# An elementwise loss kernel: its loads and stores moved from one DMA queue to three, in chunks half as large

## The chip, the cores and the metric

The kernel runs on one core of a Trainium2 chip. The metric is device time in microseconds (us); lower is better. Nearly all executions are in one undisturbed ("fast") state; the one run of an experiment that was not is named where it occurs, and two experiments had a single run each, whose state is unknown.

A core has 16 DMA engines that move data between HBM (the memory outside the core) and the on-chip SBUF, and compute engines of which two matter here: DVE (VectorE) and ACT (ScalarE). DMAs can be issued by GpSimd (called POOL in the profile), by SyncE (SP) and by ACT. Each issuer has its own queue.

## The reference

```python
# pred, target: (8192, 8192) float32; target holds 0.0 or 1.0
def reference(pred, target):
    eps = 1e-7
    pred = np.clip(pred, eps, 1 - eps)
    return -(target * np.log(pred) + (1 - target) * np.log(1 - pred))
```

As a target is 0 or 1, the result is -ln|t - 1 + p|. Each of the three arrays has 268.4 MB, and each element is used once.

## The kernel before

Each array is seen as 128 rows (partitions) of 524288 columns, and cut into chunks. A chunk of width w is a contiguous piece of HBM, so a row of it is one run of w elements: 16384 float32 values are 64 KiB. Chunks live in two rings in SBUF. The prediction tile is computed on in place and stored from there. The target load casts float32 to bfloat16 on the way.

```python
RING = 32768
SUB = 2048
def chunk_widths(total):
    head = [4096, 4096, 8192]
    tail = [8192, 4096, 2048, 1024, 1024]
    big = 16384
    ...
ring_p = pool.tile([P, RING], fp32, ...)
ring_t = pool.tile([P, RING], bf16, ...)

def load(k):
    c, w = at(k), widths[k]
    nc.gpsimd.dma_start(out=ring_t[:, c : c + w], in_=dram(target_f, cols[k], w))
    nc.gpsimd.dma_start(out=ring_p[:, c : c + w], in_=dram(pred_f, cols[k], w))
def store(k):
    c, w = at(k), widths[k]
    nc.gpsimd.dma_start(out=dram(out_f, cols[k], w), in_=ring_p[:, c : c + w])
def front(c, w):   # DVE: clip; t - 1 + p.  ACT: abs; ln        (each in place)
    ...
def back(c, w):    # DVE: times -1
    ...
def compute(k):    # pieces of SUB columns; back runs one piece behind, within the chunk
    ...
# main loop, cut: a store is issued when the next load needs its place in the ring
for k in range(len(widths)):
    while loaded < len(widths):
        end = cols[loaded] + widths[loaded]
        while stored < k and end > cols[stored] + RING:
            store(stored); stored += 1
        if end > cols[stored] + RING:
            break
        load(loaded); loaded += 1
    compute(k)
```

So there is one DMA queue, GpSimd's, in which targets, predictions and results follow each other, and the ring holds two large chunks.

Of the kernel before, what the change touches and what calls it, by code (L numbers as in the profile page):

```python
# [1 line left out]

# [4 lines left out]

EPS = 1e-7



RING = 32768

SUB = 2048


def chunk_widths(total):
    head = [4096, 4096, 8192]
    tail = [8192, 4096, 2048, 1024, 1024]
    big = 16384  # L20
    n = (total - sum(head) - sum(tail)) // big
    widths = head + [big] * n + tail
    assert sum(widths) == total
    return widths


@with_exitstack
def kernel(
    ctx: ExitStack,
    tc: tile.TileContext,  # L30
    pred: bass.AP,
    target: bass.AP,
    out: bass.AP,
):






    nc = tc.nc
    fp32 = mybir.dt.float32
    bf16 = mybir.dt.bfloat16
    Alu = mybir.AluOpType
    Act = mybir.ActivationFunctionType
    P = nc.NUM_PARTITIONS

    R, C = pred.shape
    pred_f = pred.rearrange("r c -> (r c)")
    target_f = target.rearrange("r c -> (r c)")  # L50
    out_f = out.rearrange("r c -> (r c)")
    total = R * C // P

    def dram(flat, col, w):
        return flat[col * P : (col + w) * P].rearrange("(p w) -> p w", p=P)

    pool = ctx.enter_context(tc.tile_pool(name="rings", bufs=1))
    ring_p = pool.tile([P, RING], fp32, name="ring_p", tag="ring_p")
    ring_t = pool.tile([P, RING], bf16, name="ring_t", tag="ring_t")
    warm = pool.tile([1, 8], fp32, name="warm", tag="warm")  # L60
    nc.vector.memset(warm, 1.0)  # L61
    nc.scalar.activation(out=warm, in_=warm, func=Act.Ln)  # L62

    widths = chunk_widths(total)
    cols = [sum(widths[:k]) for k in range(len(widths))]

    def at(k):
        c = cols[k] % RING
        assert c + widths[k] <= RING
        return c  # L70

    def load(k):
        c, w = at(k), widths[k]
        nc.gpsimd.dma_start(out=ring_t[:, c : c + w], in_=dram(target_f, cols[k], w))  # L74
        nc.gpsimd.dma_start(out=ring_p[:, c : c + w], in_=dram(pred_f, cols[k], w))  # L75

    def store(k):
        c, w = at(k), widths[k]
        nc.gpsimd.dma_start(out=dram(out_f, cols[k], w), in_=ring_p[:, c : c + w])  # L79

    def front(c, w):
        p, t = ring_p[:, c : c + w], ring_t[:, c : c + w]
        nc.vector.tensor_scalar(  # L83
            out=p, in0=p, scalar1=EPS, scalar2=1 - EPS, op0=Alu.max, op1=Alu.min
        )
        nc.vector.scalar_tensor_tensor(  # L86
            out=p, in0=t, scalar=1.0, in1=p, op0=Alu.subtract, op1=Alu.add
        )
        nc.scalar.activation(out=p, in_=p, func=Act.Abs)  # L89
        nc.scalar.activation(out=p, in_=p, func=Act.Ln)  # L90

    def back(c, w):
        p = ring_p[:, c : c + w]
        nc.vector.tensor_scalar(  # L94
            out=p, in0=p, scalar1=-1.0, scalar2=None, op0=Alu.mult
        )

    def compute(k):
        c, w = at(k), widths[k]
        n = max(1, w // SUB)  # L100
        s = w // n
        for i in range(n):
            front(c + i * s, s)
            if i:
                back(c + (i - 1) * s, s)
        back(c + (n - 1) * s, s)



    with tc.manual_schedule():  # L110
        stored = loaded = 0
        for k in range(len(widths)):
            while loaded < len(widths):
                end = cols[loaded] + widths[loaded]
                while stored < k and end > cols[stored] + RING:
                    store(stored)
                    stored += 1
                if end > cols[stored] + RING:
                    break
                load(loaded)  # L120
                loaded += 1
            compute(k)
        while stored < len(widths):
            store(stored)
            stored += 1


# [1 line left out]
_INS = ['pred', 'target']  # L129
_OUTS = [((8192, 8192), 'float32')]  # L130


# [23 lines left out]
```

## Time and profile before

| | before |
|---|---|
| time, median of 3 runs | 1870.75 us |
| DMA engines busy, 100 to 1840 us | 100% |
| DVE / ACT busy | 63% / 52% |
| bytes through the engines, counted on the wider side | 805.3 MB |

From the page of the kernel before: busy time of the compute engines; the busy tenths of the 16 DMA engines in 40 slices; the queue with its packets, MB and share of the span of 16 engines; the HBM traffic.

```profile
DVE 1178.6 (63%) x772; ACT 976.3 (52%) x516; POOL 65.4 (3%) x118
...
DMA  9999999999999999999999999999999999999998
...
q0 software_dynamic: 16416, 671.10, 99.9%
...
HBM read 536.87 MB, written 268.44 MB: 431 GB/s over the span
```

The waits view of the kernel before (who waited for whom; us in total, times, longest us). L75 is the prediction load, L83 the clip, L86 t - 1 + p, L89 the abs:

```profile
POOL ring_p L75 <- DMA out_dram<-ring_p: 1084.9, 30, 37.1
ACT ring_p L89 <- DVE ring_p L86: 876.0, 222, 23.7
...
DVE ring_p L83 <- DMA ring_p<-in_pred_dram: 552.9, 32, 18.8
```

The windows view of the kernel before: the long middle, then the last 29 us. After the busy times of DVE, ACT and POOL come the TensorE clock (of no use here), the DMA share, and GB/s.

```profile
100.00:1840.00 1740.00, 1113.56 (x727) 922.12 (x485) 55.68 (x98) 1.00 1.00 361
1840.00:1869.00 29.00, 10.92 (x10) 10.49 (x8) 2.56 (x4) 1.00 0.70 301
```

How to read this. The waits are long, but the DMA share is 1.00 all through the middle. The 361 GB/s count targets at their bfloat16 size.

One step deeper, the trace keeps a record for each DMA packet. Packets are put down to one engine here by joining a packet's end to the next one's start. One engine of the kernel before (start in ns of the records' own clock, duration in ns, bytes on the SBUF side):

```
 980128  2418  65536     prediction or result, 64 KiB
 982542     9      4     a semaphore
 982550  2431  32768     target: 64 KiB read, 32 KiB written
 984962  2432  32768
  ...
1001853    22      4
1001856  2431  65536     first plain packet after a target
1004283  2418  65536
```

Successive starts are 2414 ns apart for plain packets and 2413 ns for targets, so an engine takes 27.15 GB/s *of the wider side*, with nothing in between.

### The profile page before, as it was taken

How to read it: one execution, taken by the hardware profiler on the slowest of the kernel's cores; microseconds unless marked ns; L12 is line 12 of the kernel's file. 1: busy time of each engine (PE TensorE's matmuls, PEld its weight loads, DVE VectorE, ACT ScalarE, POOL GpSimd, SP SyncE). 2: the span in 40 equal slices, each digit the busy share in tenths (PEclk: the TensorE clock that was granted, in tenths of full speed). 3: DMA queues.
4: the chain of work that ended last, by engine and by line, in shares of the span. 5: the costliest groups of instructions: out<-in, count | busy, mean ns of one | idle time of the engine just before them, and what ended most of it. 6: DMA issues, size and time to landing. Idle time of an engine off the chain costs nothing.

```text
span 1868.8 us, 1563 instructions
## 1 busy us (share of the span) xinstructions
DVE 1178.6 (63%) x772; ACT 976.3 (52%) x516; POOL 65.4 (3%) x118
## 2 busy tenths in 40 slices
DVE  4557755577555775557755577555776556755595
ACT  3446544565444654446544466444664446644474
POOL 1000000000000000000000000000000000000010
DMA  9999999999999999999999999999999999999998
GB/s 292 359 358 338 348 400 371 337 355 342 393 386 339 341 352 387 384 351 339 345 386 389 351 344 337 383 395 344 352 344 365 400 358 339 354 355 395 374 335 349
DMA packets 16427, 671.19 MB, mean 359 GB/s; under 512 B 1824, under 2 KB 1824, under 8 KB 2720
## 3 DMA queue, kind: packets, MB, share of 16 engines
q0 software_dynamic: 16416, 671.10, 99.9%
q14 instruction: 11, 0.09, 0.0%
HBM read 536.87 MB, written 268.44 MB: 431 GB/s over the span
## 4 chain that ended last, share of the span: by engine, by line
DMA 34%; issue 30%; DVE 27%; ACT 7%; POOL 1%; another core or an unknown queue 1%; POOLq 0%; PEldq 0%
DMA ring_p<-in_pred_dram 32%; DVE ring_p L86 13%; DVE ring_p L94 7%; DVE ring_p L83 7%; ACT ring_p L89 3%; ACT ring_p L90 3%; DMA out_dram<-ring_p 2%; POOL out_dram L79 1%; POOL ring_t L74 1%; POOL ring_p L75 0%; POOLq L151 0%; POOLq L79 0%; PEldq L151 0%
## 5 line engine op out<-in xcount | busy, mean ns | idle before, releaser
L89 ACT ACTIVATE ring_p<-ring_p 128x2048 f32<-128x2048 f32 (+1 forms) x257 | 488.9, 1902 | 876.0 <-DVE ring_p L86 876.0
L83 DVE TENSOR_SCALAR ring_p<-ring_p 128x2048 f32<-128x2048 f32 (+1 forms) x257 | 312.9, 1218 | 552.9 <-DMA ring_p<-in_pred_dram 552.9
L86 DVE SCALAR_TENSOR_TENSOR ring_p<-ring_t,ring_p 128x2048 f32<-128x2048 bf16 (+1 forms) x257 | 586.9, 2284 | 8.8
L90 ACT ACTIVATE ring_p<-ring_p 128x2048 f32<-128x2048 f32 (+1 forms) x257 | 489.2, 1903 | 8.1
L94 DVE TENSOR_SCALAR ring_p<-ring_p 128x2048 f32<-128x2048 f32 (+1 forms) x257 | 313.1, 1218 | 120.8 <-ACT ring_p L90 120.8
L75 POOL DMA_DIRECT2D ring_p<-in_pred_dram x38 | 21.9, 576 | 1094.1 <-DMA out_dram<-ring_p 1084.9
L79 POOL DMA_DIRECT2D out_dram<-ring_p x38 | 22.1, 581 | 700.3 <-DVE ring_p L94 689.9
L74 POOL DMA_DIRECT2D ring_t<-in_target_dram x38 | 21.8, 574 | 5.3 <-DMA ring_t<-in_target_dram 4.4
L62 ACT ACT_TABLE_LOAD x1 | 1.3, 1283 | 0.7 <-PEq L140 0.7
L61 DVE MEMSET warm<- 1x8 f32 x1 | 0.1, 65 | 0.8 <-PEq L140 0.8
L62 ACT ACTIVATE warm<-warm 1x8 f32<-1x8 f32 x1 | 0.2, 207 | 0.0
L140 POOL MEMSET const-float32-0.0<- 128x1 f32 x1 | 0.1, 98 | 0.2 <-issue 0.2
L140 POOL MEMSET const-bfloat16-1.0<- 128x1 bf16 x1 | 0.1, 101 | 0.0
L140 POOL MEMSET const-float32-1.0<- 128x1 f32 x1 | 0.1, 98 | 0.0
L140 POOL MEMSET const-uint8-127<- 128x1 uint8 x1 | 0.1, 98 | 0.0
## 6 DMA issues: line engine op xcount, KB each, us to landing
ring_t<-in_target_dram POOLq DMA_DIRECT2D x30, 4096.0 KB, 55.6
ring_p<-in_pred_dram POOLq DMA_DIRECT2D x2, 4096.0 KB, 29.1
out_dram<-ring_p POOLq DMA_DIRECT2D x2, 4096.0 KB, 30.7
ring_p<-in_pred_dram POOLq DMA_DIRECT2D x3, 2048.0 KB, 20.9
out_dram<-ring_p POOLq DMA_DIRECT2D x3, 2048.0 KB, 53.1
ring_t<-in_target_dram POOLq DMA_DIRECT2D x2, 2048.0 KB, 37.9
ring_t<-in_target_dram POOLq DMA_DIRECT2D x3, 1024.0 KB, 16.5
ring_p<-in_pred_dram POOLq DMA_DIRECT2D x1, 1024.0 KB, 30.7
```

Source lines behind the costliest of these rows:

```text
L61: nc.vector.memset(warm, 1.0)
L62: nc.scalar.activation(out=warm, in_=warm, func=Act.Ln)
L74: nc.gpsimd.dma_start(out=ring_t[:, c : c + w], in_=dram(target_f, cols[k], w))
L75: nc.gpsimd.dma_start(out=ring_p[:, c : c + w], in_=dram(pred_f, cols[k], w))
L79: nc.gpsimd.dma_start(out=dram(out_f, cols[k], w), in_=ring_p[:, c : c + w])
L83: nc.vector.tensor_scalar(out=p, in0=p, scalar1=EPS, scalar2=1 - EPS, op0=Alu.max, op1=Alu.min)
L86: nc.vector.scalar_tensor_tensor(out=p, in0=t, scalar=1.0, in1=p, op0=Alu.subtract, op1=Alu.add)
L89: nc.scalar.activation(out=p, in_=p, func=Act.Abs)
L90: nc.scalar.activation(out=p, in_=p, func=Act.Ln)
L94: nc.vector.tensor_scalar(out=p, in0=p, scalar1=-1.0, scalar2=None, op0=Alu.mult)
L140: nc = _bacc.Bacc("TRN2", target_bir_lowering=False, num_devices=1)
```

## The change

The intent: predictions, targets and results each get a queue of their own (SyncE, GpSimd, ACT), so that none stands behind another; chunks are 8192 wide (runs of 32 KiB in float32), so that the ring holds four; the negation runs LAG = 2 pieces behind, across chunk ends; the first loads are issued before anything else.

```diff
+LAG = 2
 def chunk_widths(total):
-    head = [4096, 4096, 8192]
-    tail = [8192, 4096, 2048, 1024, 1024]
-    big = 16384
+    head = [4096, 4096]
+    tail = [4096, 2048, 1024, 1024]
+    big = 8192
 ...
+    def load_t(k):
         nc.gpsimd.dma_start(out=ring_t[...], in_=dram(target_f, cols[k], w))
-        nc.gpsimd.dma_start(out=ring_p[...], in_=dram(pred_f, cols[k], w))
+    def load_p(k):
+        nc.sync.dma_start(out=ring_p[...], in_=dram(pred_f, cols[k], w))
     def store(k):
-        nc.gpsimd.dma_start(out=dram(out_f, cols[k], w), in_=ring_p[...])
+        nc.scalar.dma_start(out=dram(out_f, cols[k], w), in_=ring_p[...])
 ...
+    with tc.manual_schedule():
+        load_what_fits()              # then the warm-up of ACT's table
+        for i in range(len(pieces) + LAG):
+            if i < len(pieces):
+                front(piece i)
+            if i >= LAG:
+                back(piece i - LAG)
+                if last of its chunk:
+                    store(k); stored = k + 1; load_what_fits()
```

(Cut and shortened at "..." and in the last loop.)

More of the change, by code (lines that the diff above doesn't have):

```diff
@@ L60 @@
     warm = pool.tile([1, 8], fp32, name="warm", tag="warm")
-    nc.vector.memset(warm, 1.0)
-    nc.scalar.activation(out=warm, in_=warm, func=Act.Ln)
     widths = chunk_widths(total)
@@ L70, in at @@
         return c
-    def load(k):
+    def load_t(k):
         c, w = at(k), widths[k]
         nc.gpsimd.dma_start(out=ring_t[:, c : c + w], in_=dram(target_f, cols[k], w))
-        nc.gpsimd.dma_start(out=ring_p[:, c : c + w], in_=dram(pred_f, cols[k], w))
+    def load_p(k):
+        c, w = at(k), widths[k]
+        nc.sync.dma_start(out=ring_p[:, c : c + w], in_=dram(pred_f, cols[k], w))
     def store(k):
         c, w = at(k), widths[k]
-        nc.gpsimd.dma_start(out=dram(out_f, cols[k], w), in_=ring_p[:, c : c + w])
+        nc.scalar.dma_start(out=dram(out_f, cols[k], w), in_=ring_p[:, c : c + w])
     def front(c, w):
@@ L96, in back, with load_what_fits @@
         )
-    def compute(k):
-        c, w = at(k), widths[k]
+    pieces = []
+    for k, w in enumerate(widths):
         n = max(1, w // SUB)
-        s = w // n
         for i in range(n):
-            front(c + i * s, s)
-            if i:
-                back(c + (i - 1) * s, s)
-        back(c + (n - 1) * s, s)
-    with tc.manual_schedule():
-        stored = loaded = 0
-        for k in range(len(widths)):
-            while loaded < len(widths):
-                end = cols[loaded] + widths[loaded]
-                while stored < k and end > cols[stored] + RING:
-                    store(stored)
-                    stored += 1
-                if end > cols[stored] + RING:
-                    break
-                load(loaded)
-                loaded += 1
-            compute(k)
-        while stored < len(widths):
-            store(stored)
-            stored += 1
+            pieces.append((k, at(k) + i * (w // n), w // n, i == n - 1))
+    stored = 0
+    loaded = 0
+    def load_what_fits():
+        nonlocal loaded
+        while (
+            loaded < len(widths)
+            and cols[loaded] + widths[loaded] <= (cols + [total])[stored] + RING
+        ):
+            load_t(loaded)
+            load_p(loaded)
+            loaded += 1
+    with tc.manual_schedule():
+        load_what_fits()
+        nc.vector.memset(warm, 1.0)
+        nc.scalar.activation(out=warm, in_=warm, func=Act.Ln)
+        for i in range(len(pieces) + LAG):
+            if i < len(pieces):
+                _, c, w, _ = pieces[i]
+                front(c, w)
+            if i >= LAG:
+                k, c, w, last = pieces[i - LAG]
+                back(c, w)
+                if last:
+                    store(k)
+                    stored = k + 1
+                    load_what_fits()
 _INS = ['pred', 'target']
```

## The prediction

> **What bounds the kernel now.** The 16 DMA engines. In the windows view their share is 1.00 from 100 to 1840 us; the queue table puts queue 0 at 99.9% of 16 engines' span. DVE is busy 63% and ACT 52% (page, part 1). The large waits in the waits view (GpSimd 1084.9 us for stores to land, DVE 552.9 us for predictions) are instructions waiting behind busy DMA engines, not gaps in the transfers.
>
> The kernel moves 3 x 268.4 = 805.3 MB, counted on the wider side (the page counts targets at their bf16 size, hence its 359 GB/s). In the trace's packet records an engine moves a 64 KiB run every 2414 ns and a target run (64 KiB read, 32 KiB written) every 2413 ns, back to back, also where a store follows a load. That is 27.15 GB/s for each engine. The Trainium skill, page "DMA: Bandwidth & Descriptors", section "Where 436 GB/s comes from", gives 435 GB/s as the fabric ceiling: 805.3 MB would take 1850 us (estimate); the trace agrees, at 99.8% of that rate within a run. So of 1868.8 us only about 18 are not bare transfer: roughly 6 us of packet cost, 3 us at the start, 9 us at the end (windows view: DMA share 0.70 over the last 29 us).
>
> **What the change does.**
> - Three queues for one. The same page, section "Issuing engines are not separate DMA queues", says they run on the same 16 engines and interleave. The trace of before has one data queue and can't show this; I take it as true. No bandwidth is gained. GpSimd's waits disappear or move to SyncE; they cost nothing now.
> - 32 KiB runs for 64 KiB. Packets per engine go from about 910 to 1630. From the records a packet costs 4-5 ns above its bytes and a semaphore packet about 8 ns: +4 us (estimate).
> - Interleaving: the first plain packet after a target packet takes 2431 instead of 2418 ns. After each of some 540 target packets that is +7 us; if the queues hide it, 0.
> - Four chunks of 8192: a chunk's DMA time is 29 us, a slot lives (load up to 29, wait for the next chunk because of LAG about 29, two pieces 8, store 10-29) 76-95 us of 116 us for four. So a prediction load should always be ready, and the engines stay full. Stores on ACT wait for DVE's negation, but ACT has 48% slack.
> - Ends: loads issued before the warm-up, small stores overlapping remaining work: -4 us.
>
> **Sum.** 1870.75 + 4 (packets) + 3 (half of the interleaving cost) - 4 (ends) - 1 (rest) = about 1872 us; range 1863 to 1884. Nothing removed lies on the critical path, which is the engines' byte rate. Chances: faster by over 2% 0.01, within 2% 0.92, slower by over 2% 0.07.
>
> **What would show it.** DMA share 1.00 in the middle, about 430 GB/s of HBM traffic; 32 KiB packets near 1213 ns when alone; three queues in the queue table; DVE's waits for predictions again about 550 us in sum; DMA share in the last 29 us above 0.70.
>
> **What would make it wrong.** HWDGE cutting runs into smaller packets (at 4 KiB, 4-5 ns each would add 35 us); switching between queues, or between reading and writing, leaving bubbles; target loads running ahead so that predictions starve and DVE, waiting for the next chunk before it negates the last, delays stores until the queues run dry; or queues overlapping inside an engine, which would beat the 1850 us floor.

## The result and the profile after

The changed kernel took 1874.63 us, the median of 4 runs (1874.35 to 1877.65), against 1870.88 (1870.64 to 1871.72) for the kernel before in the same rounds. The ratio is 1.0023, interval 1.0006 to 1.0040. A ratio is the mean time of one kernel's fast runs over that of the other's of the same rounds, so it isn't quite the ratio of the medians. The small loss is clear of the noise. The profiled run was the slowest of the four, 1877.65 us.

From the page of the changed kernel, the lines that answer to those of before:

```profile
DVE 1175.1 (63%) x772; ACT 980.0 (52%) x516; POOL 63.0 (3%) x72
...
DMA  9999999999999999999999999999999999999998
...
q1 hardware_dynamic: 9792, 268.44, 33.6%
q0 software_dynamic: 9792, 134.22, 33.5%
q10 hardware_dynamic: 9792, 268.44, 33.2%
...
HBM read 536.87 MB, written 268.44 MB: 429 GB/s over the span
```

Its waits view, where L75 is the target load, L87 the clip, L90 t - 1 + p and L93 the abs, then one line of the waits view for SyncE's queue, where L79 is the prediction load:

```profile
POOL ring_t L75 <- DVE ring_p L90: 1681.9, 62, 32.2
ACT ring_p L93 <- DVE ring_p L90: 878.3, 256, 16.3
DVE ring_p L87 <- DMA ring_p<-in_pred_dram: 599.4, 64, 11.1
DVE ring_p L90 <- DMA ring_t<-in_target_dram: 83.3, 39, 11.8
```

```profile
SPq L79 <- DMA out_dram<-ring_p: 1783.0, 61, 63.7
```

Its windows view, the middle and the last 29 us:

```profile
100.00:1840.00 1740.00, 1102.67 (x722) 918.49 (x482) 57.16 (x60) 1.00 1.01 360
1847.00:1876.00 29.00, 11.97 (x11) 8.05 (x6) 0.00 (x0) 1.00 0.76 309
```

What to see: three queues share the engines in equal thirds of the time, although the targets' queue 0 shows half the MB of the others: its bytes on the wider side are the same. GpSimd's wait for stores has become SyncE's wait for stores. The middle moves 360 GB/s where it moved 361. The work has been rearranged, the rate has not.

The records of one engine show the price of the sharing (start, duration, bytes on the SBUF side, queue: 10 result, 0 target, 1 prediction):

```
1000215  1213  32768  10
1001425  1226  16384   0
1002632  1226  32768   1
1003854  1213  32768  10
1005063  1226  16384   0
```

An engine changes queue after every packet, and one packet is one run of 32 KiB. A result takes 1210 ns from start to start, a target 1207, and the prediction after the target 1222: 3639 ns for the three. The bytes alone, at the 435 GB/s that the Trainium skill's page "DMA: Bandwidth & Descriptors" gives as the ceiling, would be 3614 (estimate), so 25 ns are cost.

A steady rate can be summed from these records. Over 300 to 1500 us of the profiled run of each kernel, with every packet counted on its wider side:

| kernel | rate in the middle, GB/s | 805.3 MB at that rate, us | median time, us | the rest, us |
|---|---|---|---|---|
| before | 433.96 | 1855.7 | 1870.9 | 15.2 |
| changed | 431.94 | 1864.4 | 1874.6 | 10.2 |

The changed kernel loses 8.7 us to a lower rate, and gets 5.0 us back outside of it. "The rest" is a remainder: median time minus what all the bytes would take at the middle's rate. (The profiled run of the changed kernel was 3 us longer than its other runs. The 3 us are not in the middle: the run without compute below has the same transfers and was profiled at 1874.05 us, and it moves 432.0 GB/s in the middle too. The two differ by at most 0.5 us of transfers until 1855 us, and then in the last 20 us; why is open.) The experiments ask what the two terms consist of.

### The profile page after: what moved, and what is told of

The parts are those of the page before. It is cut to its first block, busy times and chain, and to the rows that moved or that the text cites. A ratio compares the mean times of both kernels' runs of the same rounds, so it can differ in the third digit from the quotient of the medians.

```text
span 1875.9 us, 1857 instructions
## 1 busy us (share of the span) xinstructions
DVE 1175.1 (63%) x772; ACT 980.0 (52%) x516; POOL 63.0 (3%) x72
## 4 chain that ended last, share of the span: by engine, by line
DMA 85%; DVE 13%; another core or an unknown queue 1%; issue 0%; ACT 0%; SPq 0%; POOL 0%; DVEq 0%; PEldq 0%
DMA out_dram<-ring_p 45%; DMA ring_p<-in_pred_dram 37%; DVE ring_p L90 6%; DVE ring_p L87 4%; DVE ring_p L98 3%; DMA ring_t<-in_target_dram 3%; ACT ring_p L93 0%; SPq L79 0%; POOL ring_t L75 0%; ACT ring_p L94 0%; DVEq L90 0%; PEldq L163 0%
## 5 line engine op out<-in xcount | busy, mean ns | idle before, releaser
L93 ACT ACTIVATE ring_p<-ring_p 128x2048 f32<-128x2048 f32 (+1 forms) x257 | 489.4, 1904 | 878.3 <-DVE ring_p L90 878.3
L87 DVE TENSOR_SCALAR ring_p<-ring_p 128x2048 f32<-128x2048 f32 (+1 forms) x257 | 313.2, 1219 | 599.4 <-DMA ring_p<-in_pred_dram 599.4
L90 DVE SCALAR_TENSOR_TENSOR ring_p<-ring_t,ring_p 128x2048 f32<-128x2048 bf16 (+1 forms) x257 | 587.1, 2284 | 92.1 <-DMA ring_t<-in_target_dram 83.3
L75 POOL DMA_DIRECT2D ring_t<-in_target_dram x68 | 62.8, 925 | 1682.7 <-DVE ring_p L90 1681.9
```

What stands on the lines that cost most here:

```text
L87: nc.vector.tensor_scalar(out=p, in0=p, scalar1=EPS, scalar2=1 - EPS, op0=Alu.max, op1=Alu.min)
L90: nc.vector.scalar_tensor_tensor(out=p, in0=t, scalar=1.0, in1=p, op0=Alu.subtract, op1=Alu.add)
L93: nc.scalar.activation(out=p, in_=p, func=Act.Abs)
```

## The experiments

The theory: the time is the wider-side bytes through 16 engines, plus a few ns for each packet, plus some ns for each switch out of a target packet, plus the ends. Rivals: the ring's chain of waits or the compute sets the pace; the engines are bound by bytes on the SBUF side; the shorter runs or the three queues carry the whole difference.

### The bytes: half the results, and no compute

```diff
-nc.scalar.dma_start(out=dram(out_f, cols[k], w), in_=ring_p[:, c : c + w])
+nc.scalar.dma_start(out=dram(out_f, cols[k], w)[:, : w // 2],
+                    in_=ring_p[:, c : c + w // 2])
```

> Wrong result on purpose: each store writes only the first half of its columns (16 KiB runs), all else stays. Theory (bytes through the 16 engines): 134.2 MB less at 27.15 GB/s for each of 16 engines is 309 us less: about 1566 us. Rival (the loads alone set the time, e.g. by HBM reads at a fixed rate): little change. Rival 2 (the chunk period is set by the ring's chain of waits): between.

Measured: 1570.45 us (1570.07 to 1570.64), with nan where nothing was written. The 134.2 MB that were left out took 304 us with them: the theory's 309, nearly. DVE, ACT and the two loads did all of their work in 1570 us, so neither sets the time at 1874.

```diff
 def front(c, w):
-    clip (DVE), abs and ln (ACT)
     p = t - 1 + p        (DVE, kept: it reads both tiles)
-            back(c, w)
```

> Wrong result on purpose: of the compute only the one DVE instruction that reads both tiles is left (p = t - 1 + p), all transfers stay. Theory (DMA engines bound it, compute only shows at the end): about 3-6 us less than the changed kernel, 1869-1872 us. Rival (DVE's 600 us of waits for predictions or its chunk-end coupling hold back the transfers): more than 20 us less.

Measured: 1874.15 us. Its output is wrong, which doesn't matter for the time. Taking away all of ACT's work and two of DVE's three instructions (clip and negation) gained about 0.5 us by the medians (1.4 us when each is set against the kernel before of its own rounds). Three to six were expected at the end, so that part missed, but the rival is out by far. The waits view of this run, where L87 is the one DVE instruction left:

```profile
POOL ring_t L75 <- DVE ring_p L87: 1714.6, 62, 31.0
DVE ring_p L87 <- DMA ring_t<-in_target_dram: 1298.0, 68, 20.6
```

DVE's wait just grew by the work that it no longer had. A wait of an engine that isn't the bottleneck is only the room it has left.

### Which side's bytes: the cast taken away

Float32 targets need more room, so the ring has three chunks here; a control has the ring of three alone.

```diff
-RING = 32768
+RING = 24576
```

> The changed kernel with a ring of three 8192-wide chunks instead of four, else the same; it is the control for the next run. A slot lives 76-95 us by the prediction's estimate, three slots give 87 us at 29 us each: at the edge, so 1875-1950 us. If the engines stay full, 1874-1878.

```diff
+RING = 24576
-ring_t = pool.tile([P, RING], bf16, name="ring_t", tag="ring_t")
+ring_t = pool.tile([P, RING], fp32, name="ring_t", tag="ring_t")
```

> Targets loaded as f32 without the cast, still by GpSimd, in a ring of three (f32 needs the room). Theory (the engines are bound by the bytes of the wider side, and a cast saves nothing): the same as the control run with a ring of three, or up to 6 us less, as the switch out of a cast packet (11-13 ns each) goes; the page's GB/s rises to about 430. Rival (the engines are bound by the bytes at SBUF, 359 GB/s as the page counts them): 134 MB more, +374 us.

Measured: 1941.94 us for the control, 1943.65 without the cast. The DMA totals of the page, first of the control, then of the run without the cast:

```profile
DMA packets 29391, 671.22 MB, mean 346 GB/s; under 512 B 3264, under 2 KB 3264, under 8 KB 4160
```

```profile
DMA packets 29391, 805.44 MB, mean 414 GB/s; under 512 B 3264, under 2 KB 3264, under 8 KB 4032
```

20% more bytes reach SBUF in the same time. So a casting load is paid for on its wider side, and 671 MB was the wrong number to divide by. In every transfer here the wider side is the HBM side, so "HBM-side bytes" would fit these runs as well. A limit that all 16 engines share, such as the HBM's rate, is another rival that no run tests; the packet records speak against it. In the last microseconds of the kernel before, a store packet of 8 KiB took 309 ns with one or two engines at work, and 309 ns with all 16. Whether the cost of switching out of target packets is gone without the cast can't be read from these times, as three chunks don't keep the engines at their rate.

The control says that the ring of four was needed: three chunks cost 67 us. Yet its windows view shows full DMA engines:

```profile
400.00:1200.00 800.00, 476.35 (x312) 397.44 (x208) 24.99 (x26) 1.00 1.00 345
```

The share is 1.00, the rate 345 instead of 360. In the records, prediction packets take 1290 ns on average instead of 1225, the slowest hundredth over 2100: the same bytes take longer, and the whole duration counts as busy. Why three chunks slow the packets down is open. So a DMA share of 1.00 alone doesn't prove that the engines run at their rate; GB/s has to be read beside it.

### The packets: shorter runs

```diff
-    big = 8192
+    big = 4096
```

> The changed kernel with 4096-wide chunks (16 KiB runs). Theory: the cost of a triplet beyond its bytes is 3639 - 3614 = 25 ns whatever its size; twice the triplets, 512 more per engine, give +13 us, and 190 more DMAs at 6-8 ns each +1.4 us: about 1889 us. Rival (the +3.8 us come from the ring and the schedule, not from packets): 1874 or less, as eight slots only loosen the ring.

```diff
-    big = 8192
+    big = 2048
```

> The changed kernel with 2048-wide chunks (8 KiB runs, 254 chunks). Theory: 25 ns for each triplet whatever its size: against 32 KiB runs 1536 more triplets, +38 us, and some 570 more DMAs at 6-8 ns, +4 us: about 1916 us. If it is well above, issue or landing latency of small DMAs comes in; if below, part of the 25 ns scales with bytes.

Measured: 1888.17 us (1888.11 to 1888.40) and 1917.61 (1917.51 to 1917.66), both within 2 us of what was expected. The middle's rates were 428.73 and 422.66 GB/s, so all the bytes took 14.0 and 40.9 us longer than in the changed kernel, for 512 and 1536 more triplets of packets on each engine: 27 ns a triplet, semaphores included, whatever the run's length. The rival (more slots help) is out.

### The queues: all three streams on GpSimd again

```diff
-nc.sync.dma_start(out=ring_p[...], in_=dram(pred_f, ...))
+nc.gpsimd.dma_start(out=ring_p[...], in_=dram(pred_f, ...))
-nc.scalar.dma_start(out=dram(out_f, ...), in_=ring_p[...])
+nc.gpsimd.dma_start(out=dram(out_f, ...), in_=ring_p[...])
```

> The changed kernel with all three streams back on the GpSimd queue (32 KiB runs, ring of four, LAG kept). Theory (packet cost plus interleaving cost minus shorter ends): the trace of the changed kernel shows a store-target-prediction triplet of packets every 3639 ns, of which about 11 ns come from the switch out of a target packet; 544 triplets x 11 ns = 6 us go, so about 1868.5 us. Rival 1 (the queues cost nothing, the whole +3.8 us is the shorter runs): stays at 1874-1875. Rival 2 (three queues help somewhere): 1878 or more.

And the kernel before, with the widths of the changed one only:

```diff
-    head = [4096, 4096, 8192]; tail = [8192, 4096, 2048, 1024, 1024]; big = 16384
+    head = [4096, 4096]; tail = [4096, 2048, 1024, 1024]; big = 8192
```

> The kernel before with only the widths of the changed one (8192-wide chunks, same head and tail). Theory: about 720 more packets per engine at 4-5 ns and 90 more semaphore packets at 6-8 ns give +4 us: about 1875 us; no interleaving, so target packets follow each other at about 1207-1209 ns. If the shorter tail (one 8192 chunk fewer) helps at the end, 1871-1873. Rival 1: the same 1874.6 as the changed kernel.

Measured: 1880.88 us for the first (five fast runs, 1878.01 to 1885.43; a sixth took 1927.84) and 1879.89 for the second (1878.03 to 1881.90). The ratios to the kernel before are 1.0055 (1.0042 to 1.0068) and 1.0049 (1.0037 to 1.0061). Both expectations failed: one queue was to be about 6 us faster than three, and is about 6 us slower. Rival 2 of the first run, "three queues help somewhere", was right. The rates show where:

| kernel | rate in the middle, GB/s | 805.3 MB at that rate, us | median time, us | the rest, us |
|---|---|---|---|---|
| before | 433.96 | 1855.7 | 1870.9 | 15.2 |
| before, 8192-wide chunks | 431.78 | 1865.1 | 1879.9 | 14.8 |
| changed, one queue | 432.74 | 1860.9 | 1880.9 | 20.0 |
| changed (three queues) | 431.94 | 1864.4 | 1874.6 | 10.2 |

In undisturbed stretches of the middle the theory held. An engine needs, from one undisturbed chunk to the next, 57959 ns for 16384 columns in the kernel before, so 28980 for 8192; with one queue and 32 KiB runs it needs 29046. That is the packet cost: 66 ns x 64 chunks = 4.2 us. With three queues the mean is 29131: another 85 ns x 64 = 5.4 us, or 11 ns for each target packet, the interleaving. Single-queue runs also have packets that take some hundred ns longer now and then, in bursts, and these eat up most of the gain. The 8192-wide run before has such a burst at 950 to 1100 us, and its mean rate is no better than that of three queues. The one-queue run has one after 1500 us, outside the table's window: over 300 to 1780 us it moves 432.30 GB/s, so that all bytes take 1862.8 us and the rest is 18.1 us (the other rows change by 0.3 us at most). So in these profiled runs three queues cost 1.7 us against one queue, or nothing. What stretches those packets is open.

At the ends the one-queue kernel loses about 8 us to the three-queue one (18.1 against 10.2). Three parts are seen in the traces, in single profiled runs:
- Its first data packet starts 2.6 us into the span, against 1.7 with the prediction loads on SyncE.
- After the last data it takes longer to close. The waits view of SyncE's queue, one queue first, then three, shows the closing barrier as "PEq":

```profile
SPq L163 <- PEq L163: 4.4, 2, 3.9
```

```profile
SPq L163 <- PEq L163: 0.7, 2, 0.5
```

  In the one-queue kernel GpSimd joined this barrier 3.8 us after SyncE, though all data had landed. The kernel before with 8192-wide chunks shows the same 3.9 us, the kernel before itself only 0.4; there, the last store was issued alone, 4 us before the end. The trace's record of GpSimd is one instruction of the closing, DRAIN: it begins at 1845.3 us with the last store's issue and ends at 1878.4, 4 us after the last landing. In the kernel before, it ends 0.4 us after the last landing. What DRAIN waits for is not in the profile.
- Its engines don't finish together: the 16 completions of its last store are spread from 1870.6 to 1874.3 us, the last engine 2.6 us behind the other 15, as the stores were queued without a break up to the end. In the kernel before they lie within 0.2 us, as all engines had run dry beforehand. In the changed kernel they lie within 0.7 us.

What is left of the 8 us was not taken apart.

### The ring of two, with three queues

```diff
-    head = [4096, 4096]; tail = [4096, 2048, 1024, 1024]; big = 8192
+    head = [4096, 4096, 8192]; tail = [8192, 4096, 2048, 1024, 1024]; big = 16384
```

> The changed kernel's three queues and LAG with the widths of the kernel before (16384-wide chunks, so a ring of two; 64 KiB runs). Theory: a store waits for two pieces of the next chunk (LAG), the next load for that slot waits for the store: store 21 + load 39-41 + two pieces 9 = about 71 us a chunk against 58 us of transfer, so the engines run dry: 2050-2250 us. Rival (free queues keep the engines full with any ring): about 1870.

Then the same, but with a chunk's negations done before the next chunk begins:

```diff
-        for i in range(len(pieces) + LAG):
-            ... back(piece i - LAG) ...
+        for k, c, w, last in pieces:
+            front(c, w)
+            pend.append((k, c, w, last))
+            while len(pend) > (0 if last else LAG):
+                finish()     # back of the oldest; if last: store, load_what_fits
```

> As the run with a ring of two, but the negations of a chunk are finished before the next chunk's first piece, so a store no longer waits for the next load. Theory: slot = load 39-58 + compute 41 + store 21 = 101-120 us against 2 x 58 = 116: near full, 1865-1960 us. Rival (the ring of two, not the LAG, starves the engines): as slow as the run before this one.

Measured, one run each (state unknown): 2116.38 and 2258.29 us. The first is as expected: from the trace, stores are issued every 66 us, where transfers need 58. The second expectation failed, and the LAG is not what starves the engines. In the DMA view of both (issue to landing, median us, of the large chunks; first with LAG, then without), the store tells why:

```profile
ring_t<-in_target_dram POOLq DMA_DIRECT2D x30, 4096.0 KB, 36.1
ring_p<-in_pred_dram SPq DMA_DIRECT2D x30, 36.1
out_dram<-ring_p ACTq DMA_DIRECT2D x30, 20.7
```

```profile
ring_t<-in_target_dram POOLq DMA_DIRECT2D x30, 4096.0 KB, 51.8
ring_p<-in_pred_dram SPq DMA_DIRECT2D x30, 50.0
out_dram<-ring_p ACTq DMA_DIRECT2D x30, 46.5
```

With the LAG, a store comes when no load is under way, has the engines to itself and lands in 20.7 us; the ring gets its slot back soon. Without it, stores run at the same time as the other slot's loads, and all three share the engines packet by packet, so each takes 46 to 52 us. Everything that the next step waits for lands late, then both slots compute and the engines idle. This is a reading of two traces, not a separate test; that stores which share are slower is in the numbers, that it is the whole of the 142 us is not shown. It does show why a split into free queues needs the deeper ring, and so the shorter runs.

### An attempt to beat both: the ends alone

The middle of the kernel before is close to the engines' rate, so only its ends were altered: first prediction loads and last stores on SyncE, and the last five chunks pipelined across chunk ends.

```diff
-nc.gpsimd.dma_start(out=ring_p[...], in_=dram(pred_f, ...))
+(nc.sync if k < 2 else nc.gpsimd).dma_start(out=ring_p[...], in_=dram(pred_f, ...))
+first_tail = len(widths) - 5
+    ... for k >= first_tail: back one piece behind, across chunks, then
+        nc.sync.dma_start(out=dram(out_f, cols[k], w), in_=ring_p[:, c : c + w])
```

> The kernel before, one GpSimd queue with 64 KiB runs in the middle, and only its ends altered: the first two prediction loads and the last five stores on the SyncE queue, and the compute of the last five chunks pipelined across chunk ends. Theory: the middle is at the byte rate and only the ends can gain; the last store of before was issued 2.9 us after its data were ready and DVE and ACT had gaps between the small chunks, so about -4 to -6 us: 1865-1867 us. Rival (the ends are bounded by latencies that this does not touch): 1869-1871.

Measured: 1859.08 us, but the result was wrong (nan): `c` and `w` were those of the chunk's last piece, so part of two chunks was never written. A time with missing stores proves nothing. Mended:

```diff
-        nc.sync.dma_start(out=dram(out_f, cols[k], w), in_=ring_p[:, c : c + w])
+        nc.sync.dma_start(out=dram(out_f, cols[k], widths[k]),
+                          in_=ring_p[:, at(k) : at(k) + widths[k]])
```

> The run with altered ends again, its fault mended: there the last five stores used the column and width of a chunk's last piece, so two of them wrote only 2048 columns and 8192 columns of 128 x 4 bytes (4.2 MB, 9.7 us of the engines) were never written; its 1859.1 us doesn't count. Theory (the middle at the byte rate, about 1856 us of packets; ends: first packet at 1.7 instead of 2.6 us, no last store held back on GpSimd): 1859 + 9.7 of missing stores, of which 2-4 us fit into the 4.7 us that the engines stood idle in its last 15 us: 1864-1867 us, so 0.2-0.4% below the kernel before, clear of the changed kernel's 1874.6. Rival (the ends are bounded by latencies that this does not touch): 1869-1871.

Measured: 1868.90 us (1868.14 to 1869.14), correct; ratio to the kernel before 0.9988 (0.9974 to 1.0001). So it gains perhaps 2 us on the kernel before, with an interval that just reaches 1, and it is faster than the changed kernel by 5.7 us (medians of different rounds). Less was gained than expected: its last 29 us in the windows view are better filled than before (0.78 against 0.70), but not full:

```profile
1837.00:1866.00 29.00, 9.47 (x9) 9.38 (x7) 0.00 (x0) 1.00 0.78 336
```

Yet all stores were issued by 1849.4 us. The completions of its last store are spread from 1859.4 to 1865.5 us: the engines end up to 6 us apart, and the kernel ends with the last of them. The drift isn't made by the tail: the spread of one transfer's 16 completions grows through the whole run, from 0.4 us near 30 us to 6.0 near 1770. It does so in the kernel before as well (0.6 to 6.3 us). In the changed kernel it goes up and down between 2 and 6 us, and is below 1 us at the end. Why engines drift, and why three queues bring them together again, was not tested.

## Why the prediction was right

- **The bound.** It named the byte rate of the 16 engines on the wider side. Half the results less took 304 us away, the whole of ACT's work 0.5 us, and 20% more SBUF bytes cost 2 us.
- **No bandwidth from three queues.** Right: 431.94 GB/s in the middle against 433.96. The Trainium skill, page "DMA: Bandwidth & Descriptors", section "Issuing engines are not separate DMA queues", was taken on trust for this; the three equal shares and the alternating packets now show it.
- **Packets, +4 us.** Measured 4.2 us in undisturbed stretches, and the law of a fixed cost for each packet held down to 8 KiB runs.
- **Interleaving, +3 us, as half of a possible 7.** Against undisturbed stretches with one queue the trace has 5.4 us: the queues hide little of it. Against whole single-queue runs with 32 KiB runs it is 1.7 us or nothing, as their stretched packets make up for it; these were not foreseen. In sum the middle lost 8.7 us where 7 were forecast.
- **Ends and rest, -5 us.** Measured -5.0 as a remainder. Of the two reasons given, the profiled run shows 0.9 us (first data packet at 1.7 us instead of 2.6) and 1.7 us (DMA share 0.76 instead of 0.70 over the last 29 us). What makes up the other 2.4 us in ordinary runs no profile shows, so that the sum agrees this well is partly luck. That the closing of the kernel takes longer after a full GpSimd queue was not foreseen either; it plays no part between these two kernels (0.4 and 0.5 us), and showed when one queue was slower than three.
- **The ring.** "76-95 us of 116" meant that four slots suffice. Four do; three cost 67 us (about 30.4 us a chunk at the 345 GB/s of its middle, so 91 us for three).
- **What the profile would show.** HBM 429 GB/s, three queues, a DMA share of 0.76 in the last 29 us, all as said. DVE's waits for predictions came to 599 us instead of 550, with 83 more for targets.

1872 was forecast, 1874.6 measured. The follow-up theory from the same numbers, one queue being 6 us faster, was wrong, because it took the ends to be the same.

## What to carry to other kernels

When the DMA engines run back to back, count the bytes on the wider side of each transfer, divide by the rate that one packet shows, and see how much is left before splitting queues: here it was under 1%. Splitting a stream over queues doesn't add rate; it costs a little at each switch, makes each transfer land later because all share, and so needs a deeper ring. Here its gains were at the start and at the end, and altering just the ends of the kernel before got about half of them (the rest fell from 15.2 to about 13 us) without the loss in the middle: 1868.9 us against 1874.6.

## What the Trainium skill lacked or had wrong

- "DMA: Bandwidth & Descriptors", section "Queues, rings and completion order", says that an engine drains a packet of typically 9-17 descriptors before it switches queue. Here the records show a switch after every single run of 32 KiB (1213 or 1226 ns each); how many descriptors such a run is they don't say.
- The same page, section "Issuing engines are not separate DMA queues", says that concurrent issue saves only the sequencer's time. Here it cost 11 ns for each target packet (5.4 us) in undisturbed stretches, and the kernel with all streams on GpSimd was 6 us slower, with 3.9 instead of 0.5 us in the closing barrier. No page has either.
- The same page says that a cast needs GpSimd, not what it costs. Here a float32 to bfloat16 load costs its float32 bytes: 2413 ns for 64 KiB read and 32 KiB written, as for a plain 64 KiB.
- "SBUF — State Buffer", in its summary for kernel authors, advises about 358 GB/s for transfers between HBM and SBUF, without asking whether the core streams alone. This core, with the other cores not running this program, moved 434 GB/s in the middle. That agrees with the 435 GB/s ceiling of "DMA: Bandwidth & Descriptors", section "Where 436 GB/s comes from", and not with the remark there that the HBM side (about 358) binds such transfers. Other pages of the skill already allow a core that streams alone more.
- The skill warns in general that busy shares mislead for DMA, but no page has a measured case: the ring of three showed 1.00 at 345 GB/s, the ring of four 1.01 at 360.
- The skill says that the 16 engines finish independently, but no page says how far they can drift apart: 6.0 us by the end of the last run (1859.4 to 1865.5 us).
